# Three edits to a two-layer decoder trunk: gating products on GpSimd, v's first loads issued later, two sets of PSUM banks at the end

## The chip, the cores and the metric

The kernel runs on one core of a Trainium2 chip. The metric is the device time of one execution in microseconds (us), lower is better. A profiled execution gives a trace: what each engine did and when, counted from the start of its span. The engines are PE (TensorE, the matrix multiplier; its weight loads are listed as PEld), DVE (VectorE), ACT (ScalarE), POOL (GpSimd) and SP (SyncE, which here only issues DMAs). Each engine takes its own instructions strictly in the order in which the program was built.

## The reference

Two layers over a residual stream `x` of 1024 positions by 2048 channels, all in float32. Cut to what is computed:

```python
for layer in range(2):
    mod = silu(c) @ w_mod[layer] + b_mod[layer]            # 2048 x 6144, a matrix-vector product
    shift, scale, gate = split(mod, 3)
    h = rms_norm(x, ln_pre_g[layer]) * (1 + scale) + shift
    y = ab_mixer(h) if layer == 0 else ssm_mixer(h)
    x = x + gate * rms_norm(y, ln_post_g[layer])

def ab_mixer(h):                                           # layer 0
    a_u, a_v, a_z, q, k, v, b_z = split(h @ w_in, 7)       # 2048 x 7168
    # 8 gating heads: chunks of 128 positions mixed by a masked 128 x 128 matrix
    vh = rms_norm(gelu(a_v) per head);  s = tril(w_s) @ vh + b_s
    out_a = gelu(a_u) * s * silu(a_z)
    # 8 stick-breaking attention heads, strictly causal
    z = q k^T / sqrt(128);  later = reversed cumulative sum of log_sigmoid(-z)
    out_b = (exp(log_sigmoid(z) + later) masked) @ v * silu(b_z)
    return concat(out_a, out_b) @ w_out                    # 2048 x 2048

def ssm_mixer(h):                                          # layer 1
    u, z = split(h @ w_in, 2)                              # 2048 x 2048
    y = S5 state space of u (64 groups of 16 channels, 64 complex states) + d * u
    g = gelu(y);  y = g * sigmoid(g @ w_glu + b_glu)       # 1024 x 1024
    return (y * silu(z)) @ w_out                           # 1024 x 2048
```

## The kernel before, in words

Every large product is done with three matmuls (`mm3`, L209 to L212): each float32 operand is split into a high part (ACT copies it to fp32r, `whi`) and a remainder (DVE subtracts, `wlo`), by `split` (L186, L187). `gemm` (from L214) walks over the contraction: `load_w` takes a raw weight tile `wraw` from a ring of four, splits it, and four PSUM banks accumulate. In the last step the banks are finished one after the other, and `evac` empties each. The banks come from `mm_tile`, a set of four, unless the caller hands in `tiles`.

The order of the work. A scheduler builds the instruction order of each engine from the program text, from priorities (`hi_prio`) and from its own timeline; `tc.issue_after(x)` keeps instructions behind `x` in that order, and `tc.manual_schedule` keeps the written order on the engines it names. The stages are:

1. Modulation of layer 0 and the first projections (up to about 146 us). SP loads four x tiles `xa` of 1 MB, then `w_mod` in pieces of 1 MB (`ring` and `raw`, L371; two pieces make up what one round of `sums`, L380, needs) and the first weights `fraw`. PE forms the modulation row from these, ACT and DVE turn it into the normalised, transposed `hTh` and `hTl` (high and low), and PE runs the first three projections (`first`).
2. Eight heads (to about 1600 us). Each head `h` has projections (`v`, `qk`, `uz`, `bz`), the stick-breaking attention, and a gating head. `proj_v(0, 0)` (L466) is the first of the projections of v. `gate_a(h)` runs the silu and gelu functions on ACT and then calls `sgu_out(h)` (L545): the product `sg` times `u` (L547), then that times `zg` into `u` in another order of its elements (L548), then a store to `cat_d` (L550). In heads 0 to 2 the rest of the modulation (`mod_chunk`) is done beside it on DVE, in heads 3 to 7 the preparation of the S5 matrices (`s5_prep`), whose products are on POOL (L1159, L1162), its transposes and small matmuls on PE (`wb_ps` L1285, `k_ps` L1298).
3. Output projection of layer 0 (`o0e`, `o1e`), projections of layer 1, S5 blocks.
4. The two last stages: the GLU product (`glue`, four column groups, each with eight split weights), and the output projection of layer 1 (`out0e` with four column groups of 512, `out1e` with three, and `outr`, the fourth for the last four row blocks, kept apart so that each row block ends with its own normalisation `post` and store). `outr` takes its weights from `wres`, split once.

In the last stage `evac` (L963) empties a bank twice: DVE multiplies it by the gains into `y` (L965), ACT squares it for the norm (`jk`, L967).

Of the kernel before, what the change touches and what calls it, by code (L numbers as in the profile page):

```python
# [63 lines left out]
def hybrid_trunk(ctx: ExitStack, tc: tile.TileContext, x, c, ln_pre_g, ln_post_g, w_mod, b_mod,  # L64
# [10 lines left out]
    def pool(name, bufs=1, **kw):  # L75
        return tc.tile_pool(name=name, bufs=bufs, reuse_waits="tile", **kw)
# [10 lines left out]
    def big_tile(i, shape, dt, name):  # L87
        return big[i].tile(shape, dt, tag="big", name=name)
# [183 lines left out]
    def perm(t):  # L272
        return t.rearrange("p (j n) -> p n j", j=8)
# [40 lines left out]
    with pool("p0") as p0:  # L314
# [148 lines left out]
        hTh[1] = big_tile(1, [128, KT, 512], F32R, "hTh1")  # L463
        hTl[1] = big_tile(1, [128, KT, 512], F32R, "hTl1")
        new_v()
        proj_v(0, 0)  # L466
        xbank = [ps_z.tile([128, 512], F32, tag="z", name="xT") for _ in range(2)]
        with hi_prio():
            for k in range(KT):
# [6 lines left out]
    with pool("pa") as pa, pool("pst") as pst, pool("pat", 2) as pat, ExitStack() as pm_stack:  # L476
# [67 lines left out]

        def sgu_out(h):  # L545
            u, z, s = st["u"], st["z"], st["s"]
            V.tensor_tensor(out=s, in0=s, in1=u, op=ALU.mult)  # L547
            V.tensor_tensor(out=perm(u), in0=s.rearrange("p (n j) -> p n j", j=8),  # L548
                            in1=z.rearrange("p (n j) -> p n j", j=8), op=ALU.mult)
            dma(out=cat_d[h], in_=u)  # L550

# [152 lines left out]
    def proj_z(cg, halves, pre=None):  # L704
# [12 lines left out]
        o = 1024 + cg * 256  # L717
        gemm(KT, 256, lambda k0, k1: [(0, 0, wi[:, k0:k1, o:o + 256])], banks, evac, f"sz{cg}e", pre)

    with pool("pb") as pb:  # L720
        gg = pb.tile([128, D], F32, name="gg0")
        dma(out=gg, in_=gg_d[0].partition_broadcast(128))
# [6 lines left out]
        def load_cat(hf, k):  # L729
            with hi_prio():  # L730
                raw = load_raw(kord(catv, k, slice(hf * 512, (hf + 1) * 512)), 512)
                split(catH[hf][:, KORD[k], :], catL[hf][:, KORD[k], :], raw)

        def other_banks(name):

            return [p_.tile([128, 512], F32, tag=tag, name=name)
                    for p_, tag in ((ps_z, "z"), (ps_z, "z"), (ps_t, "t"), (ps_o, "o"))]

        def h1_turn(hf, ys, ks):

# [172 lines left out]
    with pool("pe") as pe:  # L913
        wg = w_glu[0].rearrange("(k p) n -> p k n", p=128)
        zs = []
        tab.begin("sigm")
        for k in range(8):
            zt = pe.tile([128, L], F32, tag="zt", name="zt", bufs=8)
            dma(out=zt, in_=z_d[k])
            gt = pe.tile([128, L], F32, tag="gt", name="gt", bufs=2)  # L920
            dma(out=gt, in_=g_d[k])
            G.tensor_tensor(out=gt, in0=gt, in1=zt, op=ALU.mult)  # L922
            tab.act(zt, zt, AF.Sigmoid)
            V.tensor_tensor(out=zt, in0=zt, in1=gt, op=ALU.mult)
            zs.append(zt)
        for cg in range(4):
            def evac(b, ps, cg=cg):
                cb, hf = divmod(b, 2)
                k = cg * 2 + cb
                s = slice(hf * 512, (hf + 1) * 512)  # L930
                sg = pe.tile([128, 512], F32, tag="sgm", name="sgm", bufs=3)
                tab.act(sg, ps, AF.Sigmoid, bias=BGLU[:, k:k + 1])
                V.tensor_tensor(out=sg, in0=sg, in1=zs[k][:, s], op=ALU.mult)
                split(yTh[:, k, s], yTl[:, k, s], sg)

            banks = []
            for cb in range(2):
                for hf in range(2):
                    def f(k, wh, wl, cb=cb, hf=hf):
                        s = slice(cb * 128, (cb + 1) * 128)  # L940
                        t = slice(hf * 512, (hf + 1) * 512)
                        return wh[:, s], wl[:, s], gT[0][:, k, t], gT[1][:, k, t]
                    banks.append((512, f))
            gemm(8, 256, lambda k0, k1, cg=cg: [(0, 0, wg[:, k0:k1, cg * 256:(cg + 1) * 256])], banks, evac, "glue")
        tab.begin("explog")


    with pool("pd") as pd:
        gg = pd.tile([128, D], F32, name="gg1")
        dma(out=gg, in_=gg_d[1].partition_broadcast(128))  # L950
        wo2 = w_out_ssm[0].rearrange("(k p) n -> p k n", p=128)
        outv = out[0].rearrange("(n j) d -> j n d", j=8)

        def op_out(k, wh, wl, j):
            s = slice(j * 128, (j + 1) * 128)
            return yTh[:, k, s], yTl[:, k, s], wh, wl

        for hf in range(2):
            js = range(hf * 4, hf * 4 + 4)
            ys = [pd.tile([128, D], F32, tag="y", name="y1", bufs=4) for _ in js]  # L960
            ssq = pd.tile([128, 4, 4], F32, tag="ssq", name="ssq1", bufs=2)

            def evac(b, ps, ng, ys=ys, ssq=ssq):  # L963
                n0 = ng * 512
                V.tensor_tensor(out=ys[b][:, n0:n0 + 512], in0=ps, in1=gg[:, n0:n0 + 512], op=ALU.mult)  # L965
                jk = pd.tile([128, 512], BF16, tag="jk", name="jk1")
                S.activation(jk, ps, AF.Square, accum_out=ssq[:, b, ng:ng + 1])  # L967

            def post(b, n, ys=ys, ssq=ssq, js=js, hf=hf):
                tot = pd.tile([128, 1], F32, tag="tot", name="tot1", bufs=2)  # L970
                V.tensor_reduce(out=tot, in_=ssq[:, b, :], axis=mybir.AxisListType.X, op=ALU.add)
                r = rstd_from(tot, 1, D, pd, "ry")
                for q in range(D // n):
                    qs = slice(q * n, (q + 1) * n)
                    xr = pd.tile([128, 1024], F32, tag="xr", name="xr1", bufs=4)[:, 0:n]
                    dma(out=xr, in_=x1_d[js[b]][:, qs])
                    o = ys[b][:, qs] if hf else xr
                    V.scalar_tensor_tensor(out=o, in0=ys[b][:, qs], scalar=r, in1=xr, op0=ALU.mult, op1=ALU.add)
                    (G.dma_start if n > 512 else dma)(out=outv[js[b]][:, qs], in_=o)

            for ng in range(4 if hf == 0 else 3):
                banks = [(512, lambda k, wh, wl, j=j: op_out(k, wh, wl, j)) for j in js]
                gemm(8, 512, lambda k0, k1, ng=ng: [(0, 0, wo2[:, k0:k1, ng * 512:(ng + 1) * 512])], banks,
                     lambda b, ps, ng=ng, evac=evac: evac(b, ps, ng), f"out{hf}e")
            if hf == 0:
                for b in range(4):
                    post(b, 1024)
            else:
                wres = big_tile(0, [128, 2, 8, 512], F32R, "wres")
                for k in range(8):  # L990
                    with hi_prio():
                        raw = load_raw([(0, 0, wo2[:, k:k + 1, 1536:2048])], 512)
                        split(wres[:, 0, k, :], wres[:, 1, k, :], raw)
                for b, j in enumerate(js):
                    ps = mm_tile("outr")
                    for k in range(8):
                        mm3(ps, *op_out(k, wres[:, 0, k, :], wres[:, 1, k, :], j), k == 0, k == 7)
                    evac(b, ps, 3)
                    post(b, 1024 if b < 3 else 512)
# [344 lines left out]
```

## Time and profile before

| | |
|---|---|
| median of 3 runs | 2652.79 us (2651.98 to 2653.84) |
| the profiled execution | 2647.22 us |
| its span | 2645.5 us |
| PE busy | 2581.9 us, 98% of the span |
| DVE busy | 1556.2 us, 59% |
| ACT busy | 1017.9 us, 38% |
| POOL busy | 373.2 us, 14% |
| mean granted TensorE clock | 0.997 of full |

The profiled execution is one of its own, 5.6 us under the median of the others, and 1.7 us of it lie outside the span. A busy PE need not be a fast one, since matmuls overlap, but where PE is listed idle nothing of the kernel's main work goes on. So the idle time of PE and what released it is what to read. Idle time of the other engines costs nothing by itself.

### The profile page before, as it was taken

Reading aid. Unit: us, or ns where it says so; the run is one execution under the profiler, and the core shown is the slowest. Engines: PE = TensorE matmul, PEld = TensorE weight load, DVE = VectorE, ACT = ScalarE, POOL = GpSimd, SP = SyncE. Lnnn points to the kernel's source line nnn. Section 1 sums busy time; section 2 is a strip of 40 time slices with the busy share of each in tenths; the row PEclk is TensorE's granted clock in tenths of the full one; section 3 lists DMA queues with packets and bytes.
Section 4 is the critical chain, followed back from the end, with each engine's and each line's share of the span. In section 5 each row is a group of like instructions: output and inputs, shape, how many; then the busy total and the mean of one; then the engine's idle time right before and its main releaser. Section 6 shows DMA issues by size and latency. Waiting matters only on the chain.

```text
span 2645.5 us, 40197 instructions
## 1 busy us (share of the span) xinstructions
PE 2581.9 (98%) x14107; PEld 2171.6 (82%) x14107; DVE 1556.2 (59%) x3613; ACT 1017.9 (38%) x2021; POOL 373.2 (14%) x692
## 2 busy tenths in 40 slices
PE   5999999999999999999999999999999999999998
PEld 3788988988989878778889777887888888887886
DVE  1244676676756766855847664455264676646354
ACT  3384524235315315234334353444253322134333
POOL 0000101000000260631713400013013000002000
PEclk9999999999999999999999999999999999999999
DMA  9935283772752241422413435453364675463354
GB/s 348 382 92 173 65 262 107 235 251 61 250 182 73 64 117 52 129 70 76 127 50 113 108 96 187 160 201 102 96 218 148 207 229 182 139 213 137 132 204 169
DMA packets 373050, 410.75 MB, mean 155 GB/s; under 512 B 30032, under 2 KB 269424, under 8 KB 371568
## 3 DMA queue, kind: packets, MB, share of 16 engines
q1 hardware_dynamic: 364480, 390.28, 46.5%
q0 software_dynamic: 8160, 17.84, 2.0%
q8 instruction: 111, 1.82, 0.3%
q14 instruction: 91, 0.75, 0.1%
q10 hardware_dynamic: 208, 0.07, 0.0%
HBM read 348.28 MB, written 59.79 MB: 154 GB/s over the span
## 4 chain that ended last, share of the span: by engine, by line
PE 73%; issue 9%; DVE 7%; DMA 6%; ACT 3%; SPq 1%; POOL 1%; DVEq 0%; ACTq 0%; POOLq 0%
PE z L564 2%; PE oT L592 2%; PE o1e L210 2%; PE o1e L211 2%; PE o1e L212 2%; DVE wlo L187 1%; PE out0e L212 1%; PE out0e L210 1%; PE out0e L211 1%; PE su1e L210 1%; PE su1e L212 1%; PE su1e L211 1%; PE mrow L380 1%; PE su0e L210 1%; PE su0e L212 1%
## 5 line engine op out<-in xcount | busy, mean ns | idle before, releaser
L186 ACT ACTIVATE whi<-wraw 128x512 fp32r<-128x512 f32 x608 | 381.2, 630 | 928.3 <-PE o1e L212 87.3
L187 DVE TENSOR_TENSOR wlo<-wraw,whi 128x512 fp32r<-128x512 f32 x608 | 429.4, 709 | 480.2 <-ACT whi L186 469.1
L180 DVE SCALAR_TENSOR_TENSOR macc<-mraw,cond,macc 128x512 f32<-128x512 f32 x240 | 180.1, 751 | 77.4 <-DMA mraw<-in_w_mod_dram 73.1
L56 ACT ACTIVATE sp<-sp 128x128 f32<-128x128 f32 (+3 forms) x192 | 99.5, 520 | 3.6
L210 PE MATMUL o1e<-whi,catH 128*128 128x512 f32 x256 | 99.2, 391 | 1.4 <-ACT jk L765 1.4
L210 PE MATMUL o0e<-whi,catH 128*128 128x512 f32 x256 | 100.1, 391 | 0.0
L211 PE MATMUL o0e<-wlo,catH 128*128 128x512 f32 x256 | 100.0, 391 | 0.0
L212 PE MATMUL o1e<-whi,catL 128*128 128x512 f32 x256 | 99.8, 390 | 0.0
L211 PE MATMUL o1e<-wlo,catH 128*128 128x512 f32 x256 | 99.8, 390 | 0.0
L212 PE MATMUL o0e<-whi,catL 128*128 128x512 f32 x256 | 99.7, 390 | 0.0
L56 ACT ACTIVATE sp<-z 128x128 f32<-128x128 f32 (+3 forms) x96 | 46.8, 488 | 118.5 <-PE z L564 118.3
L526 POOL DMA_DIRECT2D sw<-in_sgu_w_dram x8 | 4.7, 586 | 575.9 <-PE sgw L530 380.5
L592 PE MATMUL oT<-wT,v 128*128 128x128 f32 x576 | 80.4, 275 | 5.6 <-DVE wT L590 5.6
L592 PEld LDWEIGHTS oT<-wT,v 128*128 128x128 f32 x576 | 75.1, 191 | 9.8 <-DVE wT L590 6.9
L564 PE MATMUL z<-k,q 128*128 128x128 f32 (+3 forms) x192 | 77.4, 486 | 0.0
L569 DVE SCALAR_TENSOR_TENSOR sp<-z,sp 128x128 f32<-128x128 f32 (+3 forms) x96 | 52.9, 551 | 40.9 <-ACT sp L56 40.9
L922 POOL TENSOR_TENSOR gt<-gt,zt 128x1024 f32<-128x1024 f32 x8 | 20.5, 2571 | 385.1 <-DMA gt<-g_d 379.0
L56 ACT ACTIVATE wt<-wt 128x128 f32<-128x128 f32 (+3 forms) x96 | 50.2, 522 | 58.0 <-DVE wt L581 54.8
L590 DVE COPY wT<-wT_ps 128x128 f32<-128x128 f32 (+3 forms) x96 | 53.1, 553 | 26.8 <-PE wT_ps L588 26.2
L802 POOL DMA_DIRECT2D x_d<-y x32 | 17.6, 550 | 345.9 <-DVE y L799 331.5
L1288 ACT ACTIVATE s5wb<-wb_ps 128x128 f32<-128x128 f32 x64 | 17.7, 276 | 126.3 <-DVE s5wb L1287 96.6
L571 POOL TENSOR_SCALAR_AFFINE_SELECT sp<-sp 128x128 f32<-128x128 f32 x64 | 22.8, 356 | 259.5 <-DVE sp L569 242.6
(627 smaller groups left out, 7924.6 us busy)
## 6 DMA issues: line engine op xcount, KB each, us to landing
wraw<-in_w_in_ab_dram SPq DMA_DIRECT2D x528, 128.0 KB, 2.5
mraw<-in_w_mod_dram SPq DMA_DIRECT2D x256, 256.0 KB, 3.8
wraw<-in_w_out_ab_dram SPq DMA_DIRECT2D x128, 256.0 KB, 3.1
wraw<-in_w_in_ssm_dram SPq DMA_DIRECT2D x112, 256.0 KB, 3.4
ring<-in_w_mod_dram SPq DMA_DIRECT2D x16, 1024.0 KB, 10.9
raw<-in_w_mod_dram SPq DMA_DIRECT2D x16, 1024.0 KB, 9.7
wraw<-in_w_out_ssm_dram SPq DMA_DIRECT2D x64, 256.0 KB, 3.3
wraw<-in_w_in_ab_dram SPq DMA_DIRECT2D x32, 256.0 KB, 2.8
```

The costliest lines, as they stand in the source:

```text
L56: r = self.nc.scalar.activation(out, in_, func, **kw)
L180: V.scalar_tensor_tensor(out=acc, in0=m, scalar=cond[:, k:k + 1], in1=acc, op0=ALU.mult, op1=ALU.add)
L186: S.activation(h, r, AF.Copy)
L187: eng.tensor_tensor(out=lo, in0=r, in1=h, op=ALU.subtract)
L210: T.matmul(ps, sh, mh, start=first, stop=False)
L211: T.matmul(ps, sh, ml, start=False, stop=False)
L212: T.matmul(ps, sl, mh, start=False, stop=last)
L380: T.matmul(prow[32 * j:32 * j + 32], condb[:, kk, :], m[:, k + j % 2, :], start=kk < 2, stop=kk >= KT - 2)
L564: T.matmul(z[:, :w], q[:, i * 128:(i + 1) * 128], kT[:, k0:k1], start=True, stop=True)
L569: V.scalar_tensor_tensor(out=a[:, :w], in0=z[:, :w], scalar=0.0, in1=a[:, :w], op0=ALU.max, op1=ALU.add)
L590: V.tensor_copy(wT[:, :w], pt[:, :w])
L592: T.matmul(oT, v[:, k0 // 128 + j, :], wT[:, j * 128:(j + 1) * 128], start=nb_done == 0, stop=nb_done == i)
```

## The change

It has three parts. First, `proj_v(0, 0)` is put behind the last load of `w_mod` of the modulation stage. Second, the two products of `sgu_out` are issued on POOL instead of DVE (`G` instead of `V`). Third, in the two last stages every other column group takes its banks from the pools `ps_z`, `ps_t` and `ps_o` (`other_banks`, which moves to an outer place); `wres` is loaded and split during the second column group of `out1e` instead of behind the third; `outr` uses the other banks; and in `evac` ACT's square is issued ahead of DVE's product.

```diff
         new_v()
-        proj_v(0, 0)
+        with tc.issue_after(st["last"].ins):
+            proj_v(0, 0)
...
         def sgu_out(h):
             u, z, s = st["u"], st["z"], st["s"]
-            V.tensor_tensor(out=s, in0=s, in1=u, op=ALU.mult)
-            V.tensor_tensor(out=perm(u), in0=s.rearrange("p (n j) -> p n j", j=8),
+            G.tensor_tensor(out=s, in0=s, in1=u, op=ALU.mult)
+            G.tensor_tensor(out=perm(u), in0=s.rearrange("p (n j) -> p n j", j=8),
                             in1=z.rearrange("p (n j) -> p n j", j=8), op=ALU.mult)
             dma(out=cat_d[h], in_=u)
...
+    def other_banks(name):
+
+        return [p_.tile([128, 512], F32, tag=tag, name=name)
+                for p_, tag in ((ps_z, "z"), (ps_z, "z"), (ps_t, "t"), (ps_o, "o"))]
...
-            gemm(8, 256, lambda k0, k1, cg=cg: [(0, 0, wg[:, k0:k1, cg * 256:(cg + 1) * 256])], banks, evac, "glue")
+            gemm(8, 256, lambda k0, k1, cg=cg: [(0, 0, wg[:, k0:k1, cg * 256:(cg + 1) * 256])], banks, evac, "glue",
+                 tiles=other_banks("glue") if cg % 2 else None)
...
                 n0 = ng * 512
-                V.tensor_tensor(out=ys[b][:, n0:n0 + 512], in0=ps, in1=gg[:, n0:n0 + 512], op=ALU.mult)
                 jk = pd.tile([128, 512], BF16, tag="jk", name="jk1")
                 S.activation(jk, ps, AF.Square, accum_out=ssq[:, b, ng:ng + 1])
+                V.tensor_tensor(out=ys[b][:, n0:n0 + 512], in0=ps, in1=gg[:, n0:n0 + 512], op=ALU.mult)
...
+            if hf:
+                wres = big_tile(0, [128, 2, 8, 512], F32R, "wres")
+
+            def load_res(k):
+
+                with hi_prio():
+                    raw = load_raw([(0, 0, wo2[:, k:k + 1, 1536:2048])], 512)
+                    split(wres[:, 0, k, :], wres[:, 1, k, :], raw)
+
             for ng in range(4 if hf == 0 else 3):
...
-                     lambda b, ps, ng=ng, evac=evac: evac(b, ps, ng), f"out{hf}e")
+                     lambda b, ps, ng=ng, evac=evac: evac(b, ps, ng), f"out{hf}e",
+                     load_res if hf and ng == 1 else None, tiles=other_banks(f"out{hf}e") if ng % 2 else None)
...
-                wres = big_tile(0, [128, 2, 8, 512], F32R, "wres")
-                for k in range(8):
-                    with hi_prio():
-                        raw = load_raw([(0, 0, wo2[:, k:k + 1, 1536:2048])], 512)
-                        split(wres[:, 0, k, :], wres[:, 1, k, :], raw)
+                spare = other_banks("outr")
                 for b, j in enumerate(js):
-                    ps = mm_tile("outr")
+                    ps = spare[b]
```

Since a scheduler sets the order, the change moves more than its lines. SP's queue at the start of the program, and (below the line of dots) where the modulation's loads end; `wraw` are v's weights, `xb` the second half of x:

```order
-L136 DMA xa<-in_x_dram 128x2048
-L195 DMA wraw<-in_w_in_ab_dram 128x2x128 x5
-L136 DMA xa<-in_x_dram 128x2048
-L195 DMA wraw<-in_w_in_ab_dram 128x2x128 x3
-L136 DMA xa<-in_x_dram 128x2048 x2
+L1348 UNCONDITIONAL_BRANCH
+L136 DMA xa<-in_x_dram 128x2048 x4
 L371 DMA ring_144<-in_w_mod_dram 128x8x256 x4
...
 L371 DMA raw_143<-in_w_mod_dram 128x8x256 x4
+L195 DMA wraw<-in_w_in_ab_dram 128x2x128 x8
 L460 DMA xb<-in_x_dram 128x2048 x4
```

The eight loads of v leave the place between the x tiles and stand behind the last `w_mod` load, ahead of `xb`.

POOL's queue in the fourth head, before, where the S5 preparation has begun (`s5Tr`, `s5Ti`, `s5cAr` and `s5cAi` are what PE transposes or multiplies, `s5cl` a load for the next groups):

```order
L1162 TENSOR_TENSOR s5Tr_7884<-s5Tr_7884,s5tb_7886 128x128
L1159 TENSOR_TENSOR s5tb_7886<-s5pw_7580,s5bbr_7871 128x128
L1162 TENSOR_TENSOR s5Ti_7885<-s5Ti_7885,s5tb_7886 128x128
L1232 DMA s5cl_8151<-in_c_re_dram 16x2x64 x4
L1232 DMA s5cl_8151<-in_c_im_dram 16x2x64 x2
L1159 TENSOR_TENSOR s5cAr_7887<-s5pw_7580,s5cT_7865 128x144
```

and the same place after the change (numbers of lines are 8 higher there):

```order
L1167 TENSOR_TENSOR s5tb_7886<-s5pw_7580,s5bbr_7871 128x128
L1170 TENSOR_TENSOR s5Ti_7885<-s5Ti_7885,s5tb_7886 128x128
L548 TENSOR_TENSOR sg<-sg,u 128x1024
L1240 DMA s5cl_8151<-in_c_re_dram 16x2x64 x4
L1240 DMA s5cl_8151<-in_c_im_dram 16x2x64 x2
L1167 TENSOR_TENSOR s5cAr_7887<-s5pw_7580,s5cT_7865 128x144
L1167 TENSOR_TENSOR s5tb_7886<-s5pw_7580,s5cT_7865 128x144
L1167 TENSOR_TENSOR s5cAi_7888<-s5pw_7580,s5cT_7865 128x144
...
L1240 DMA s5cl_8151<-in_c_im_dram 16x2x64 x2
L549 TENSOR_TENSOR u<-sg,zg 128x128x8
```

The two products of the gating head now stand within the chain of the S5 preparation, the first ahead of the loads `s5cl`, the second behind them. The sixth head has them in such a place too; in the other heads they stand between the masks of the attention or at the edge of the S5 work.

ACT's queue before, where `out1e` goes over into `outr`:

```order
L186 ACTIVATE whi<-wraw 128x512
L967 ACTIVATE jk_24975,ssq_24668<-out1e 128x512
L967 ACTIVATE jk_24981,ssq_24668<-out1e 128x512
L967 ACTIVATE jk_24987,ssq_24668<-out1e 128x512
L186 ACTIVATE whi<-wraw 128x512 x4
L186 ACTIVATE wres<-wraw 128x512 x8
L967 ACTIVATE jk_25129,ssq_24668<-out1e 128x512
```

After the change nothing of `wres` is left there; its eight copies stand in the second column group, in turn with those of `whi`.

## Rows read from the trace of the kernel before

**Rows 1.** The page's busy time of the engines: busy us (share) and instructions.
```profile
PE 2581.9 (98%) x14107; PEld 2171.6 (82%) x14107; DVE 1556.2 (59%) x3613; ACT 1017.9 (38%) x2021; POOL 373.2 (14%) x692
```

**Rows 2.** Waits of PE: line, released by, us in total, times, longest.
```profile
PE mrow L380 <- DMA ring<-in_w_mod_dram: 17.4, 2, 15.7
PE glue L210 <- ACT sgm L56: 1.8, 2, 1.5
```

**Rows 3.** Timeline of PE, first 48 us: start, us, instruction [idle before, released by].
```profile
24.47 3.64 PE L380 MATMUL mrow<-ring,condb 128*32 128x256 f32 x32 [15.67 <-DMA ring<-in_w_mod_dram]
...
39.72 3.64 PE L380 MATMUL mrow<-raw,condb 128*32 128x256 f32 x32 [2.02 <-DMA raw<-in_w_mod_dram]
...
47.59 1.93 PE L380 MATMUL mrow<-raw,condb 128*32 128x256 f32 x32
```

**Rows 4.** Timeline of PE behind those products: two of five such gaps.
```profile
667.84 1.05 PE L164 MATMUL cs<-ones,macc 128*128 128x1 f32 x8 [1.10 <-DVE wT L590]
...
1586.78 1.16 PE L592 MATMUL oT<-wT,v 128*128 128x128 f32 x8 [2.25 <-DVE wT L590]
```

**Rows 5.** Timeline of PE in the last stage, its two gaps.
```profile
2567.52 0.50 PE L210 MATMUL out1e<-whi,yTh 128*128 128x512 f32 x1 [1.13 <-ACT jk L967]
...
2612.71 0.50 PE L210 MATMUL outr<-wres,yTh 128*128 128x512 f32 x1 [1.37 <-ACT jk L967]
```

**Rows 6.** DMA issues of the first 12 us: queue, count, KB each, us to landing.
```profile
wraw<-in_w_in_ab_dram SPq DMA_DIRECT2D x8, 128.0 KB, 5.1
```

**Rows 7.** Timeline of SP's DMA issues, first 22 us.
```profile
1.26 5.37 SPq L195 DMA_DIRECT2D wraw<-in_w_in_ab_dram  x5
6.91 0.34 SPq L136 DMA_DIRECT2D xa<-in_x_dram  x1
7.30 1.63 SPq L195 DMA_DIRECT2D wraw<-in_w_in_ab_dram  x3
...
9.96 11.67 SPq L371 DMA_DIRECT2D ring<-in_w_mod_dram  x4
```

**Rows 8.** Stretches of the start; the last three columns: clock, DMA share, GB/s.
```profile
4.00:8.00 4.00, 0.00 (x0) 0.00 (x0) 0.00 (x0) 2.00 (x2) 0.00 (x0) 1.00 0.92 280
8.00:12.00 4.00, 0.45 (x1) 0.18 (x1) 0.29 (x1) 0.00 (x0) 0.00 (x0) 1.00 0.92 307
...
20.00:24.47 4.47, 0.00 (x0) 0.03 (x1) 2.82 (x7) 3.37 (x6) 0.00 (x0) 1.00 1.09 386
...
29.79:39.72 9.93, 5.76 (x45) 2.99 (x45) 3.39 (x8) 4.83 (x8) 0.00 (x0) 0.84 1.11 373
```

**Rows 9.** The two products: ns min/median/max, and what DVE waited for (us, times).
```profile
L547 DVE TENSOR_TENSOR sg<-sg,u x8: 1224/1226/1226, 326.4 to 1584.6; 128x1024 f32<-128x1024 f32 x8
...
  ACT u L56: 26.7, 8
```

**Rows 10.** The same of the second product.
```profile
L548 DVE TENSOR_TENSOR u<-sg,zg x8: 1955/2021/2046, 328.1 to 1586.6; 128x1024 f32<-128x1024 f32 x8
```

**Rows 11.** Timeline of DVE around the last head's products.
```profile
1584.62 1.23 DVE L547 TENSOR_TENSOR sg<-sg,u 128x1024 f32<-128x1024 f32 x1 [4.84 <-ACT u L56]
1585.76 0.37 DVE L596 TENSOR_TENSOR bz<-oT,bz 128x128 f32<-128x128 f32 x1
1586.04 0.68 DVE L590 COPY wT<-wT_ps 128x512 f32<-128x512 f32 x1
```

**Rows 12.** The only products of this size on POOL, in the GLU stage.
```profile
L922 POOL TENSOR_TENSOR gt<-gt,zt x8: 2368/2400/3346, 2377.4 to 2414.5; 128x1024 f32<-128x1024 f32 x8
```

**Rows 13.** Timeline there, of DVE and of POOL.
```profile
2389.91 0.69 DVE L187 TENSOR_TENSOR yTl<-sgm,yTh 128x512 fp32r<-128x512 f32 x1
2390.51 2.89 DVE L187 TENSOR_TENSOR wlo<-wraw,whi 128x512 fp32r<-128x512 f32 x1
...
2390.43 5.23 POOL L922 TENSOR_TENSOR gt<-gt,zt 128x1024 f32<-128x1024 f32 x2 [6.08 <-DMA wraw<-in_w_glu_dram]
```

**Rows 14.** Timeline of the fourth head: POOL's S5 chain, then PE's use of it.
```profile
913.74 2.17 POOL L1232 DMA_DIRECT2D s5cl<-in_c_re_dram  x4 [7.48 <-PE c_ps L1235]
...
927.21 0.42 POOL L1159 TENSOR_TENSOR s5tb<-s5pw,s5bi 128x128 f32<-128x128 f32 x1 [4.55 <-DVE s5cAi L1280]
...
928.98 0.41 PE L1298 MATMUL k_ps<-s5cAr,s5bd 128*32 128x128 f32 x2
```

**Rows 15.** The chain that ended last, its end: start, us, what.
```profile
2618.22 0.24 PE outr L212
...
2635.05 5.47 DMA xr<-x_d
2640.55 0.75 DVE y L978
```

More of the change, by code (lines that the diff above doesn't have):

```diff
@@ L732, in load_cat @@
                 split(catH[hf][:, KORD[k], :], catL[hf][:, KORD[k], :], raw)
-        def other_banks(name):
-            return [p_.tile([128, 512], F32, tag=tag, name=name)
-                    for p_, tag in ((ps_z, "z"), (ps_z, "z"), (ps_t, "t"), (ps_o, "o"))]
         def h1_turn(hf, ys, ks):
```

## The prediction

> **What bounds the kernel now.** I read the page's busy times first: PE is busy for 2581.9 of 2645.5 us, POOL for 373.2 [rows 1]. So a change can win only where PE is idle, some 64 us in all, or lose by making it idle. The waits of PE say for whom: most is the start, where the modulation's first matmul waits 15.67 us for `w_mod` [rows 2, 3]. Then I looked for the gaps that the three parts of the change touch: five in the heads behind the gating products [rows 4], two in `glue` of 1.8 us together [rows 2], and two in the last stage [rows 5]. The reader is to see that all of them are small beside the start, where DMA is what ends last.
>
> **Part 1, v's first loads.** Eight DMAs of 128 KB, 1.05 MB in all [rows 6], leave the place between the x tiles, and SP issues `w_mod` from 9.96 us on only because 5.37 + 1.63 us before that go to them [rows 7]. The first sums then start at 24.47 us, when their data land [rows 3]. Later the queue moves 386 GB/s [rows 8], so the bytes alone are worth 1.05 MB / 386 GB/s = 2.7 us: the lower end. The upper end is the 7.0 us of issuing. In between: from 4 to 12 us the queue moved 280 and 307 GB/s, while v's loads were in it [rows 8], some 92 GB/s x 8 us = 0.74 MB below its later rate, another 1.9 us. That makes 4.6 us, and I take 4.5.
>
> Does it last? The sums of the second round, at 39.72 us, wait for DMA as well [rows 3], with the queue at 373 GB/s in between [rows 8] and the same loads in it; so they move by the same amount. From then on the page shows PE without a wait for DMA, and everything moves with it. The normalisation of x keeps up, since its own loads come earlier too. v's loads now stand ahead of `xb`, but there they have the time of the last rounds, when both are long under way before PE is done with `first`; I cost that at nothing, and it would cost 2.7 us if `xb` were what PE waits for. One thing stays open: the rounds at 24.47 and 39.72 us take 3.64 us, the one at 47.59 us 1.93 us [rows 3], TensorE being at its lower clock level (mean granted 0.84 between 29.79 and 39.72 us [rows 8]) behind its idle time. If the earlier data move that stretch, 1.7 us come or go with it.
>
> **Part 2, the products on POOL.** Each head takes 1.23 and 2.02 us from DVE [rows 9, 10], and before them DVE stands still until the gelu of `u` is done, 26.7 us over eight [rows 9]: 52.7 us, or 6.6 us a head, in which nothing else on DVE's queue goes on. Five gaps of PE follow such a block, of 0.70 to 2.25 us and 6.2 us together, of which two are shown [rows 4]. In the last head one sees how: DVE waits 4.84 us, does one product, and only then copies the `wT` that PE needs [rows 11]. If all five go, 6.2 us are won.
>
> What comes instead? On POOL a product of this size takes 2.40 us [rows 12]. The second one writes a strided output, which on DVE makes 2.02 out of 1.23 us; on POOL the trace shows no such operation, so between 2.40 and 2.40 x 2.02 / 1.23 = 3.9 us. I take 2.40, the nearest row. Off the path that costs nothing: `s` and `u` are written again only after the next projections, and what stands behind the products on POOL's queue, the load `sw` and the masks of the next attention, is wanted after those as well; SP's store to `cat_d` moves with them. But DVE isn't freed for good: a `wlo` that ran beside such a POOL product took 2.89 us instead of 0.69 [rows 13]. So each of the 16 products may hold one DVE instruction for up to 2.2 us, 4.4 us a head in place of 6.6 us. If the gaps shrink in that ratio, 6.2 x (1 - 4.4/6.6) = 2.1 us are won, and I take that.
>
> The Trainium skill speaks against this part: GPSIMD Engine Reference, section "Performance versus the Vector engine", gives 1.96 times DVE's time for such a product, and section "Specifications" says that the SBUF interfaces are shared with VectorE where it reads two SBUF inputs. The trace agrees with both: 2.40 against 1.23 us, and the 2.89 us. By that rule alone DVE would lose what it wins, and part 2 would be worth nothing; that is the first rival below.
>
> The lower end of part 2 is a loss. In the fourth and sixth head the products stand within the S5 preparation on POOL. There POOL had 4.55 us of slack once, behind `s5cAi` [rows 14], but PE's `k_ps` follows only 1.8 us behind the end of that wait [rows 14], so a later POOL soon makes PE wait. Two products of 2.40 to 3.9 us in the way are up to 6.4 us a head, 12.8 us in both; against the 6.2 us won, that is 6.6 us lost at worst.
>
> **Part 3, the last stages.** The gaps before `glue`, 1.8 us [rows 2], and before `out1e` and `outr`, 1.13 and 1.37 us [rows 5], each wait for ACT to empty the first bank of the set that the next group reuses. With another set they need not wait: 4.3 us at most, and I take 4.0, for the rest that a new order leaves. `wres` costs the same eight copies and remainders, moved into a group in which ACT and DVE then do two of each for every step of the contraction. A step there is twelve matmuls of 0.24 us [rows 15], 2.9 us, and two loads of 128 x 512 float32, 0.52 MB in that time, are 181 GB/s, under half of the 386 that the queue moves at the start [rows 8]. If the four raw tiles run short there, PE waits again, and part 3 is worth nothing: its other end is 0. Issuing ACT's square ahead of DVE's product changes only who reads the bank first: nothing. The end, from `outr` over the last load of `xr`, 5.47 us, to the last product of DVE [rows 15], hangs on PE's row blocks and moves with them.
>
> **The sum.** 4.5 + 2.1 + 4.0 = 10.6 us. The profiled execution has 2647.22 us and would have 2636.6; the median of the runs stands 5.6 us above it, at 2652.79, and goes to 2642.2 us.
>
> **The rivals.**
> 1. *The shared port eats part 2.* DVE waits for POOL as long as it worked before, the five gaps stay. For it speaks the 2.89 us [rows 13]; against it that the copy `wT<-wT_ps` before PE's gap [rows 11] reads PSUM and a stretched instruction of that kind isn't in the trace. 4.5 + 4.0 = 8.5 us: 2644.3 us.
> 2. *The new order costs half of it back.* Every head from the third on is scheduled anew, so gaps can open anywhere, and each product that a gap of today hangs on gets new neighbours. Five new gaps like today's five, 6.2 us, leave 10.6 - 6.2 = 4.4 us: 2648.4 us, which is no change. For it speaks that PE waits for so many different releasers in the heads, `cs` and `oT` [rows 4] among them; against it that the scheduler's order of today leaves such small ones.
> 3. *Slower: the S5 preparation is held up.* POOL's products wait for gelu, 26.7 / 8 = 3.3 us each head, and take 4.8 to 6.3 us; in the four heads with S5 work behind them that is 4 x 8.1 to 4 x 9.6, 32 to 38 us, by which the transposes and small matmuls on PE's queue could come late, and PE is in order. It decides from the point at which more than 8.5 + 5.3 = 13.8 us of it reach PE, 3.5 us a head. With half, 17.5 us: 2652.8 - 8.5 + 17.5 = 2661.8 us. Against it: in two of the four the new order has the products at the edge of the S5 work, not in it.
> 4. *The change doesn't do what it says*: v's loads could still be issued early. The order shows them behind, so I give it nothing.
>
> **How the numbers follow.** What this kernel's measurement can tell from no change is about 0.2%, 5.3 us: faster is below 2647.5, slower above 2658.1. The forecast has 0.45, and the first rival 0.25; both are faster. The second has 0.20, of which I count 0.17 as no change and 0.03 as faster; the third 0.10, of which 0.08 is slower and 0.02 no change. So faster 0.73, same 0.19, slower 0.08. The likeliest one's own range: part 1 from 2.7 to 7.0, part 2 from -1 to 6.2, part 3 from 2 to 4.3, hence 2652.8 - 17.5 to 2652.8 - 3.7, 2635.3 to 2649.1 us. Toward the low end all three parts would have to be at their best, so I leave it at 2635; upward the range goes to 2654, which leaves the third rival out and a little below.
>
> **What would show it.** Right: the first `mrow` sums start near 20 us instead of 24.47; the gaps of PE before `glue`, `out1e` and `outr` are gone; the two products stand on POOL at 2.4 us, and gaps behind `wT` are fewer; POOL's busy time is 38 to 50 us up. Wrong: sums at 22 us or later (part 1 too large); `wlo` or `macc` of up to 2.9 us beside the products, with a PE gap behind (rival 1); `wb_ps` or `k_ps` waiting for POOL by several us in the fourth to seventh head (rival 3); PE waiting for `whi` or `wlo` in the second group of `out1e`.

## The result and the profile after

The changed kernel is slower: 2666.97 us median (2662.82 to 2669.43) against 2653.32 us of the kernel before measured beside it (four runs each), ratio 1.0051 with a 95% interval of 1.0036 to 1.0066. The forecast was 2642.2 us, so it has the wrong sign. The profiled execution took 2669.32 us, span 2667.5, which is 22.0 us of span above the one of before; it lies at the upper end of its runs and the one of before below all of its own, so its sums overstate the loss of the medians, 13.6 us.

The page's busy times of the kernel after, which answer to [rows 1]:

```profile
PE 2593.6 (97%) x14107; PEld 2179.5 (82%) x14107; DVE 1563.2 (59%) x3597; ACT 1015.7 (38%) x2021; POOL 411.6 (15%) x708
```

PE is busy for 11.7 us more with the same 14107 matmuls, and the rest of the 22 us, some 10 us, is idle time. POOL took on 38.4 us, the low end of the forecast. DVE lost two products a head, 26 us, and is still 7.0 us *busier* than before. Its other instructions have been stretched by 33 us in sum if those 26 us are taken off, and by 25 us against run 10 below, which leaves both products out (DVE busy 1538.1 us).

PE's waits by what released them (us in total, times, longest), after:

```profile
PE cols_ps L138 <- DMA rows<-in_b_glu_dram: 11.8, 1, 11.8
PE mrow L380 <- DMA ring<-in_w_mod_dram: 9.4, 2, 7.2
PE cs L164 <- DVE macc L180: 7.2, 4, 2.5
PE oT L593 <- DVE wT L591: 5.2, 2, 4.0
PE wb_ps L1293 <- DVE s5tp L1025: 3.0, 4, 0.9
PE k_ps L1308 <- DVE s5cAi L1288: 2.7, 2, 2.1
PE gate_ps L164 <- DVE macc L180: 1.9, 3, 0.7
...
PE out1e L210 <- ACT whi L186: 1.2, 3, 0.9
```

and before, rows not shown so far:

```profile
PE cols_ps L138 <- DMA rows<-in_b_glu_dram: 8.4, 1, 8.4
...
PE oT L592 <- DVE wT L590: 5.6, 4, 2.2
...
PE cs L164 <- DVE wT L590: 1.1, 1, 1.1
PE wb_ps L1285 <- DVE s5fin L1020: 1.0, 1, 1.0
PE k_ps L1298 <- DVE bz L596: 0.9, 1, 0.9
...
PE cs L164 <- DVE macc L180: 0.4, 1, 0.4
```

The waits at `glue`, `out1e <- jk` and `outr` [rows 2, 5] are gone, and so are 8.0 us of the 17.4 for `w_mod`, of which `cols_ps` at the very start takes back 3.4. But `oT`, which the products' move was to help, has lost hardly anything in sum, and `cs`, `gate_ps`, `wb_ps` and `k_ps` have grown by 10.4 us (5.1 before, 15.5 after, over all their releasers). These are the column sums of the modulation in heads 0 to 2, and the S5 preparation. PE's timeline after, at the places of [rows 3, 4] and at the new gaps:

```profile
19.52 3.23 PE L380 MATMUL mrow<-ring,condb 128*32 128x256 f32 x32 [7.25 <-DMA ring<-in_w_mod_dram]
...
34.78 3.64 PE L380 MATMUL mrow<-raw,condb 128*32 128x256 f32 x32 [1.84 <-DMA raw<-in_w_mod_dram]
...
555.89 1.05 PE L164 MATMUL cs<-ones,macc 128*128 128x1 f32 x8 [2.13 <-DVE macc L180]
...
693.90 1.21 PE L164 MATMUL cs<-ones,macc 128*128 128x1 f32 x8 [2.46 <-DVE macc L180]
...
1277.51 0.41 PE L1308 MATMUL k_ps<-s5cAi,s5bd 128*32 128x128 f32 x2 [2.14 <-DVE s5cAi L1288]
```

Both rounds of sums start 4.9 us earlier (24.47 and 39.72 us before). How far PE is ahead of or behind before at fixed points of the program tells where the time went: 4.24 us ahead at the first `v1e` (269.39 us before), 8.66 behind at the first `bz4e` (861.35), 21.65 behind at the first `o1e` (1751.22), and 22.12 at the end of `outr`. So heads 0 to 2 lose 12.9 us and heads 3 to 7 (with `o0e`, which ends there) another 13.0, and the stages behind change little in sum.

What DVE does before such gaps, in its timeline after:

```profile
542.07 2.33 DVE L180 SCALAR_TENSOR_TENSOR macc<-mraw,cond,macc 128x512 f32<-128x512 f32 x3 [0.96 <-DMA mraw<-in_w_mod_dram]
...
550.68 5.15 DVE L180 SCALAR_TENSOR_TENSOR macc<-mraw,cond,macc 128x512 f32<-128x512 f32 x4 [2.42 <-DMA mraw<-in_w_mod_dram]
...
667.67 2.48 DVE L187 TENSOR_TENSOR wlo<-wraw,whi 128x512 fp32r<-128x512 f32 x1 [3.93 <-ACT whi L186]
670.07 0.68 DVE L591 COPY wT<-wT_ps 128x512 f32<-128x512 f32 x1
670.67 2.26 DVE L187 TENSOR_TENSOR wlo<-wraw,whi 128x512 fp32r<-128x512 f32 x1
```

and POOL's:

```profile
667.20 2.40 POOL L548 TENSOR_TENSOR sg<-sg,u 128x1024 f32<-128x1024 f32 x1 [9.14 <-ACT u L56]
669.68 2.71 POOL L549 TENSOR_TENSOR u<-sg,zg 128x1024 f32<-128x1024 f32 x1
...
1252.94 0.46 POOL L1170 TENSOR_TENSOR s5Tr<-s5Tr,s5tb 128x128 f32<-128x128 f32 x1
1255.00 2.41 POOL L548 TENSOR_TENSOR sg<-sg,u 128x1024 f32<-128x1024 f32 x1 [1.60 <-ACT u L56]
1257.36 0.43 POOL L1167 TENSOR_TENSOR s5tb<-s5pw,s5bbr 128x128 f32<-128x128 f32 x1
```

The two `wlo` beside the products take 2.48 and 2.26 us, not 0.69, while the copy of `wT` out of PSUM between them keeps its 0.68. Four `macc` take 5.15 us beside the second head's products, where three take 2.33 without. The Trainium skill (SBUF — State Buffer, section "Who interferes with whom") says that a DVE instruction with two SBUF inputs contends with a GpSimd instruction that reads SBUF. The trace agrees, with these numbers. In the sixth head POOL waits 1.60 us for gelu and then does 2.41 us of product, while S5's next product stands behind; the step from `s5Tr` to `s5tb` was 0.08 us before:

```profile
1241.48 0.46 POOL L1162 TENSOR_TENSOR s5Tr<-s5Tr,s5tb 128x128 f32<-128x128 f32 x1
1242.02 0.42 POOL L1159 TENSOR_TENSOR s5tb<-s5pw,s5bbr 128x128 f32<-128x128 f32 x1
```

PE's longer busy time goes with its clock. Stretches of the kernel after, three of them, and one of run 9 below; the column behind the busy times is the granted clock:

```profile
558.11:561.52 3.41, 3.41 (x10) 2.67 (x9) 3.38 (x7) 0.00 (x0) 0.00 (x0) 0.50 0.80 246
1616.24:1619.65 3.41, 3.35 (x13) 3.16 (x14) 1.90 (x4) 1.67 (x3) 0.00 (x0) 0.50 0.28 95
1827.87:1834.70 6.83, 5.26 (x15) 3.88 (x16) 5.57 (x8) 3.75 (x9) 6.83 (x7) 0.50 0.00 0
...
1806.83:1813.66 6.83, 5.38 (x14) 4.04 (x15) 4.76 (x7) 2.88 (x8) 6.83 (x7) 0.50 0.00 0
```

Each of the three new gaps above is followed by 3.41 us at 0.50, which is 1.2 GHz (from 558.11, 694.64 and 1278.32 us); a fourth such stretch begins at the end of a gap of 3.96 us at 1616.30, and one of 6.83 us lies at the gaps of `h1T`. Together 20.5 us at half speed, up to 10.2 us of work. The kernel before has no such stretch between its start and its end in the profile shown. But that profile is the odd one: run 1 has 3.4 us of them there, run 4 6.8, run 3 10.2, run 10 13.7 and run 9, the fastest, 17.1 us, all without a product moved to POOL, and their PE is busy for 2.3 to 5.4 us more than before. So what the clock adds to the loss is less than these two profiles say.

### The profile page after: what moved, and what is told of

It reads as the page before. It is cut to its first block, busy times and chain, and to the rows that moved or that the text cites. A ratio compares the mean times of both kernels' runs of the same rounds, so it can differ in the third digit from the quotient of the medians.

```text
span 2667.5 us, 40202 instructions
## 1 busy us (share of the span) xinstructions
PE 2593.6 (97%) x14107; PEld 2179.5 (82%) x14107; DVE 1563.2 (59%) x3597; ACT 1015.7 (38%) x2021; POOL 411.6 (15%) x708
## 5 line engine op out<-in xcount | busy, mean ns | idle before, releaser
L187 DVE TENSOR_TENSOR wlo<-wraw,whi 128x512 fp32r<-128x512 f32 x608 | 445.0, 734 | 484.6 <-ACT whi L186 476.7
L572 POOL TENSOR_SCALAR_AFFINE_SELECT sp<-sp 128x128 f32<-128x128 f32 x64 | 23.8, 371 | 259.0 <-DVE sp L570 256.7
```

Source lines behind the costliest of these rows:

```text
L187: eng.tensor_tensor(out=lo, in0=r, in1=h, op=ALU.subtract)
L572: G.affine_select(out=a[:, w - 128:w], in_=a[:, w - 128:w], pattern=[[-1, 128]], base=0, channel_multiplier=1, compare_op=ALU.is_gt, fill=0.0)
```

## The experiments

Two theories stood at the start. A: the products on POOL cost the time, and parts 1 and 3 gain. B: part 1's early start is given back in the heads. Later the cost of part 2 was divided between O, the order made anew (with the products gone from DVE the scheduler puts PE's `cs` earlier), and C, POOL working beside DVE.

"Lost" is how far PE falls back against before between the first `v1e` and the first `bz4e` (heads 0 to 2), and from there to the first `o1e` (heads 3 to 7), one profile each; `o0e` is counted with heads 3 to 7. Six profiles whose order in heads 0 to 2 is that of before lost 0.0 to 3.6 us there (1, 3, 4, 6, 9 and 12), so less than that says nothing. Three with the products on POOL there in one and the same order lost 10.5 to 13.9 (2, 5 and after).

| run | products on POOL | median us, before beside it | ratio, 95% | lost, heads 0-2 | lost, heads 3-7 |
|---|---|---|---|---|---|
| after | all | 2666.97, 2653.32 | 1.0051 (1.0036-1.0066) | 12.9 | 13.0 |
| 1 part 1 | none | 2646.67, 2652.75 | 0.9975 (0.9964-0.9986) | 0.2 | 1.7 |
| 2 part 2 | all | 2674.47, 2652.75 | 1.0077 (1.0056-1.0099) | 13.9 | 12.0 |
| 3 part 3 | none | 2651.50, 2652.75 | 0.9994 (0.9983-1.0004) | 3.6 | 1.0 |
| 4 parts 1, 3 | none | 2645.10, 2652.75 | 0.9965 (0.9954-0.9975) | 2.2 | 2.1 |
| 5 heads 0-2 | 3 heads | 2661.42, 2652.03 | 1.0037 (1.0024-1.0050) | 10.5 | 3.2 |
| 6 heads 3-7 | 5 heads | 2664.15, 2652.03 | 1.0043 (1.0027-1.0059) | 2.9 | 14.7 |
| 7 added | added | 2667.55, 2652.03 | 1.0058 (1.0042-1.0073) | 9.8 | 6.6 |
| 8 in pieces | all, in pieces | 2676.86, 2652.03 | 1.0090 (1.0075-1.0106) | 14.4 | 13.4 |
| 9 late column | none | 2640.43, 2652.97 | 0.9955 (0.9942-0.9967) | 0.0 | 1.7 |
| 10 left out | none at all | 2651.21, 2652.97 | 0.9991 (0.9981-1.0001) | 4.4 | -2.9 |
| 11 one of two | half | 2663.34, 2652.97 | 1.0041 (1.0028-1.0055) | 6.7 | 9.5 |
| 12 behind S5 | 5 heads | 2661.19, 2651.91 | 1.0035 (1.0021-1.0049) | 0.1 | 12.0 |

**1 to 4: each part by itself.** All on the kernel before; 1 is the first hunk of the diff, 2 the second, 3 the others, 4 is 1 and 3:

```
1: +with tc.issue_after(st["last"].ins):
       proj_v(0, 0)
2: -V.tensor_tensor(out=s, ...)        +G.tensor_tensor(out=s, ...)
   -V.tensor_tensor(out=perm(u), ...)  +G.tensor_tensor(out=perm(u), ...)
3: +tiles=other_banks("glue") if cg % 2 else None      (also out0e, out1e, outr)
   +load_res if hf and ng == 1 else None
   ...
```

> Only part 1: v's first loads behind the modulation, everything else as before. Theory A (the products on POOL alone cost the time): the first sums start near 19.5 us, the 4.2 us that are left of it at 269 us stay to the end, 2653.3 - 4.2 = 2649 us. Rival B (the early start is given back in the heads): in the changed kernel PE waited for macc before gate_ps and cs with an order that was still that of before, 3.8 us between 331 and 541 us; if the modulation's later loads set that pace, the same waits are here, and the time is 2652 to 2653 us.

> Only part 2: the two products of each head on POOL. Theory A: the changed kernel lost 26 us between 265 and 1773 us, all of it by the products: 2653.3 + 26 = 2679 us, with gaps of PE at k_ps, wb_ps, cs and oT and several stretches of 3.41 us at the lower clock. Rival B: 3.8 us of it belong to part 1's early start, so 2653.3 + 22 = 2675 us, with no waits at gate_ps. Rival C (the three parts hurt together only, by a new order): 2651 to 2656 us.

> Only part 3: two sets of PSUM banks in the last two stages, the early last column of W, and ACT's square ahead of DVE's product. By the changed kernel's rows PE gains 2.4 us at glue, loses 1.1 in out1e and gains 1.7 at outr: 2653.3 - 3.0 = 2650.3 us (theory A). Rival: the last loads of the residual set the end anyway, and the gain is under 1 us: 2652.5 us or more.

> Parts 1 and 3 together, the products on DVE. Theory A: 2653.3 - 4.2 - 3.0 = 2646 us, and the half-clock stretches in the heads are gone. Rival B (part 1 given back in the heads): 2650 us.

Part 1 gains 6.1 us by the medians, part 2 loses 21.7, part 3 gains 1.3, which its interval doesn't tell from nothing. The sum, 14.3 us slower, is what was measured for all three, 13.6. Part 1 and part 3 together gain 7.7. Theory A holds. B falls: in run 1 PE loses 0.2 us in heads 0 to 2, and run 2, though its 2674.5 us is B's number rather than A's, still waits 1.5 us at `gate_ps`. One sign of A failed: run 4, with no product on POOL, has two stretches at 0.50 in the heads all the same (663.98 and 1585.57 us). Part 3 is short of its 3.0 us, and PE's waits in run 3 show where; below them one of the four, with the copy on ACT that ends it:

```profile
PE out1e L210 <- ACT whi L186: 4.3, 4, 1.7
...
2579.20 0.63 ACT L186 ACTIVATE whi<-wraw 128x512 fp32r<-128x512 f32 x1 [1.49 <-DMA wraw<-in_w_out_ssm_dram]
...
2579.89 1.19 PE L210 MATMUL out1e<-whi,yTh 128*128 128x512 f32 x4 [1.70 <-ACT whi L186]
```

ACT is idle there and waits for the raw tile's load, as it does before three of the four `whi` (1.49, 2.00 and 2.75 us); SP in turn holds loads until DVE's `wlo` gives a raw tile back (21.8 us between 2540 and 2625 us).

**5 and 6: which heads.**

```
+E = G if h < 3 else V      (run 6: h > 2)
+E.tensor_tensor(out=s, ...); E.tensor_tensor(out=perm(u), ...)
```

> Part 2 alone, but with the products on POOL in heads 0 to 2 only, those that also compute the modulation. In the run of part 2 alone PE was 13.9 us behind at the end of v4e (861 us) and another 12 us behind at o0e. If the two stretches have causes of their own, this one costs the first alone: 2653 + 14 = 2667 us. Rival: the first stretch only moves later work into a bad place, and without products in heads 3 to 7 some is caught up: 2660 us or less.

> Part 2 alone, with the products on POOL in heads 3 to 7 only, those with the S5 preparation. Theory (POOL's queue and the order of the S5 work): 2653 + 12 = 2665 us, with the waits at k_ps, wb_ps, c_ps and oT as in part 2 alone, and no wait at cs above those of before. Rival (the loss hangs on the modulation heads): under 2 us, 2655 us or less.

9.4 and 12.1 us by the medians, together 21.5 against part 2's 21.7. So there are two losses that add up, one beside the modulation and one beside the S5 preparation. Run 6 came out as expected, but for `cs`, which waits 1.8 us for `macc` against 0.4 before. Run 5 is nearer to its rival's 2660 us than to 2667, but its profile shows nothing caught up later: it has lost 10.5 us in heads 0 to 2 instead of 13.9, a difference that equal orders show as well.

**7: POOL beside DVE, with the order of before.**

```
 V.tensor_tensor(out=perm(u), ...)
+G.tensor_tensor(out=z, in0=s, in1=z, op=ALU.mult)
+G.tensor_tensor(out=perm(z), in0=s, in1=s, op=ALU.mult)     (both in the strided views)
```

> The kernel before, products on DVE, with two products of the same size and form added on POOL behind them in each head, which write z when nothing reads it any more. The order of PE and DVE is that of before up to the qk projection of head 4, so in heads 0 to 2 only the shared access and POOL's queue are tested. Theory O (the new order costs it: PE's cs stands 12 to 21 matmuls earlier than macc can be done): PE is within 1.5 us of before at the end of v4e. Theory C (the shared port: each POOL product holds one DVE instruction for some 2 us): PE is 10 us or more late there, as with part 2. For the end of the run: O 2653 to 2658 us, C 2670 us.

PE lost 9.8 us in heads 0 to 2, far above theory O's 1.5 and near C's 10, with the order of PE and DVE unchanged up to the qk projection of head 4. The time is up by 15.5 us. DVE's and PE's timelines of this run, in the second head:

```profile
553.85 2.71 DVE L187 TENSOR_TENSOR wlo<-wraw,whi 128x512 fp32r<-128x512 f32 x1
556.48 2.38 DVE L180 SCALAR_TENSOR_TENSOR macc<-mraw,cond,macc 128x512 f32<-128x512 f32 x1
```

```profile
560.49 1.05 PE L164 MATMUL cs<-ones,macc 128*128 128x1 f32 x8 [2.91 <-DVE macc L180]
```

Two instructions are held, 2.0 us by the first and 1.6 by the second, and PE stands 2.91 us at the column sums of the same chunk. In the profile of before there is little slack at this place, 0.35 us from the end of the last `macc` to `cs`:

```profile
556.14 0.75 DVE L180 SCALAR_TENSOR_TENSOR macc<-mraw,cond,macc 128x512 f32<-128x512 f32 x1
...
557.24 0.95 PE L164 MATMUL cs<-ones,macc 128*128 128x1 f32 x8
```

At the other column sums right behind a `macc` it is 0.1 to 1.5 us, and 3.05 once, so most of what holds `macc` reaches PE. Summed over heads 0 to 2, DVE's instructions took 9.9 us more in this run than the medians of the same forms before, about what PE lost; 8.6 in run 2, 3.6 in run 11, and nothing in the runs without POOL's products there.

**8: the products in pieces.**

```
+for p in range(4):  c = slice(p * 256, (p + 1) * 256)
+    G.tensor_tensor(out=s[:, c], in0=s[:, c], in1=u[:, c], op=ALU.mult)
+for p in range(4):  (the strided product likewise, 32 columns of n each)
```

> Part 2 alone, with each product on POOL cut into four of 256 columns, so that none can hold a DVE instruction for longer than some 0.7 us; PE's cs stands as early as with part 2 in the first chunks. Theory O (order): the loss up to the end of v4e stays, 10 us or more, and the time is near 2670 us. Theory C (port): the held instructions go, most of the loss with them: 2660 us or less.

By the medians it loses 24.8 us against part 2's 21.7, with intervals that overlap, so the pieces are no better. The expectation of C fails, but its premise failed too: the holding was halved and not gone (4.6 us in heads 0 to 2 by the same sum), and SP waits longer. SP's timeline of this run in the first head:

```profile
334.08 0.34 SPq L554 DMA_DIRECT2D cat_d<-u  x1
334.51 1.20 SPq L195 DMA_DIRECT2D wraw<-in_w_in_ab_dram  x2
335.80 0.99 SPq L497 DMA_DIRECT2D mraw<-in_w_mod_dram  x2
```

A piece takes 0.74 us at the median and the eight of this head 6.7, so `u` is done later, and SP, which is in order, holds the loads of `wraw` and `mraw` behind the store of `u`. The store stood at 330.19 us before and at 332.91 in run 2. DVE's `wlo` beside these pieces took 0.81 us, a `macc` 1.31. That half the holding cost as much, 14.4 us in heads 0 to 2, speaks for a second cause there, the order or the later loads; this run leaves open which.

**10 and 11: relief without POOL, and half the products.** Run 10 leaves both products out on every engine, so its output lacks the gating; run 11 moves the first alone.

```
10: -V.tensor_tensor(out=s, ...)   -V.tensor_tensor(out=perm(u), ...)
11: -V.tensor_tensor(out=s, ...)   +G.tensor_tensor(out=s, ...)
```

> The kernel before without the two products of each head, on any engine (the gated output is left out: u goes to cat_d as gelu leaves it). It shows what DVE's relief is worth with nothing on POOL in return, the upper end of part 2. Theory P (the prediction's): the five gaps go, 6.2 us, 2646 us. Theory O (the order made anew costs by itself, whatever POOL does): 2656 us or more, with PE waiting at cs, which stands 2 to 6 matmuls earlier in three chunks. Theory R (most of the loss is POOL beside DVE): between 2645 and 2653 us.

> Only the first of the two products of a head (s times u, contiguous, 2.4 us) on POOL, the second stays on DVE behind it. If the loss goes with the time that POOL works beside DVE, 2.4 of 5.1 us a head, it is half of part 2's 22 us: 2663 us. If it comes from the order made anew, it is about the whole: 2670 us or more. DVE waits for POOL here, so up to 2.4 us a head may come on top of the half, where nothing else on DVE's queue covers it.

Without any product the kernel gains 1.8 us, within its uncertainty, not 6.2; that is in theory R's range. The five gaps of the prediction are gone, in this run all of them, but others opened. PE's waits of run 10:

```profile
PE cs L164 <- DVE macc L180: 3.5, 5, 1.1
PE oT L589 <- DVE wT L587: 2.7, 1, 2.7
```

The wait at `oT` is not the one of 2.25 us [rows 4] but the next in the same head, 1.52 us before. DVE's timeline in run 10 shows what is late now:

```profile
1595.15 0.69 DVE L187 TENSOR_TENSOR catL<-wraw,catH 128x512 fp32r<-128x512 f32 x1 [1.52 <-ACT catH L186]
1595.76 0.68 DVE L587 COPY wT<-wT_ps 128x512 f32<-128x512 f32 x1
```

The copy of `wT` stands behind a remainder that waits for ACT: DVE is in order, and the free time was given to work of the next stage (three such remainders between the two copies of `wT`, two before). In heads 0 to 2 the free time went into waiting for loads. What DVE waits for ahead of `macc` (us, times, longest), before, in run 10 and after:

```profile
DVE macc L180 <- DMA mraw<-in_w_mod_dram: 73.1, 77, 2.3
DVE macc L180 <- DMA mraw<-in_w_mod_dram: 84.8, 79, 3.1
DVE macc L180 <- DMA mraw<-in_w_mod_dram: 92.0, 80, 3.3
```

The two products of three heads are 9.7 us of DVE; the wait grew by 11.7 without them. It grew by 18.9 in the changed kernel; how much of that is freed time and how much loads that come late isn't separated. `cs` stands 2 to 6 matmuls earlier in three chunks and waits 3.5 us for `macc` instead of 0.4 (with part 2, 12 to 21 matmuls earlier): part of theory O is real. In heads 0 to 2 run 10 (its order alone) lost 4.4 us and run 7 (POOL alone) 9.8, together 14.2; part 2 lost 13.9. That sum proves little: the 4.4 are just outside what equal orders lost, 3.6 at most, and no run has part 2's own order without POOL, so O's share in part 2 isn't known. Run 11 lost 10.4 us by the medians with 2.4 us of POOL a head, part 2 21.7 with 5.1: that is the half of its first expectation, the loss going with the time that POOL works, and not the 2670 us of an order made anew.

**12: products out of gelu's way.** In heads 3 to 7 the products wait in POOL's queue until the S5 work of the head is issued.

```
+tab.pool = G.tensor_tensor(...)                  (S5's own products and sums)
+with tc.issue_after(tab.pool.ins) if h > 2 else nullcontext():
+    E.tensor_tensor(out=s, ...); E.tensor_tensor(out=perm(u), ...)
```

> Products on POOL in heads 3 to 7 only, but in POOL's queue behind the S5 work of the head's pieces, so that they come long after gelu and POOL never stands waiting for it with S5 work behind. In the run with these heads PE lost 14.7 us between the ends of v4e and o0e; products beside an order that doesn't wait for gelu lost 6.6 us there. Theory Q (POOL waiting for gelu holds up the S5 work): 6 to 7 us are left, 2657 us. Rival R (any 5 us of POOL's time in the S5 chain costs as much, wherever it stands): 2664 us as before.

12.0 us are lost instead of 14.7, and the time is 9.3 us above before instead of 12.1, with intervals that overlap. POOL's own wait for gelu ahead of the products fell from 39.4 to 10.2 us, all of it in the last head, so that hold is gone, but PE's waits of this run have new names:

```profile
PE sgw L530 <- ACT s5wb L1290: 3.5, 2, 2.3
PE oT L594 <- DVE wT L592: 3.4, 1, 3.4
```

2661.19 us (2657.5 to 2664.9 by the interval) lies between Q's 2657 and R's 2664, nearer to R: most of the loss doesn't hang on POOL's wait for gelu. Whether there the held DVE or POOL's own queue weighs more stays open, since the S5 preparation uses both. In these heads the runs don't add up either: run 10 (-2.9) and run 7 (6.6) make 3.7, part 2 lost 12.0.

**9: the version that beats both.** Parts 1 and 3, products on DVE, and the last column of W loaded behind the third group, as before:

```
-load_res if hf and ng == 1 else None
+for k in range(8):  raw = load_raw(... 1536:2048 ...); split(wres[:, 0, k, :], wres[:, 1, k, :], raw)
 spare = other_banks("outr")
```

> Parts 1 and 3 with the products on DVE, but the last column of W is loaded and split where it was before, behind the third group of out1e, instead of inside the second. In the runs of part 3 PE waited for whi inside out1e, 4.3 and 3.4 us. Theory (two raw tiles a step are too many there): these waits go, glue keeps its 2.4 us and outr its 1.2 to 1.5, so with part 1's 6 us the time is 2652.5 - 6 - 3.5 = 2643 us. Rival (the sets of banks bring nothing once the column is late, since ACT empties the banks as late): 2646 us, as part 1 alone.

2640.43 us, ratio 0.9955 with 0.9942 to 0.9967: 12.5 us faster than before (8.8 to 15.4 by the interval, which holds the theory's 2643 us and not the rival's 2646). In its profile PE has no wait left in `glue`, `out1e` and `outr`, and from the first `glue` to the end of `outr` it takes 5.5 us less than before. With part 1's 6.1 us that is 11.6 of the 12.5.

Against run 4, 4.7 us by the medians for the column alone; the intervals overlap, so what is shown is that the waits for `whi` went.

## Why the prediction was wrong

**Part 1, right and a little small.** Forecast 4.5, measured 4.9 us at both rounds, and 6.1 by the medians of run 1. The clock is listed at 0.50 between 25.63 and 39.28 us, before between 36.52 and 43.35; the second round takes 3.64 us in both, so nothing came or went by it there. For the round at 24.47 us, which the prediction put at the lower level too, the profile lists 1.00, so that its 3.64 us are the clock's isn't shown.

**Part 2, wrong, and nearly the whole error lies here: -2.1 us forecast, +21.7 measured, 23.8 of the 24.8 us by which the median missed.** The failed step is "If the gaps shrink in that ratio, 6.2 x (1 - 4.4/6.6) = 2.1 us". Both sides of it fail.
- *The gain.* That the five gaps hang on DVE's products is right: in run 10 all five are gone. That they would be won is wrong, since the order is made anew with it and other instructions come late, `cs`, `c_ps` and the next `oT`, and since in heads 0 to 2 DVE then waits for `mraw` instead; run 10 gains 1.8 us, with nothing on POOL. In the changed kernel `oT`'s waits are 5.2 us in place of 5.6.
- *The cost.* The 4.4 us a head of held DVE instructions was right as a bound: the 25 to 33 us of stretching are 3 to 4 us a head, the two `wlo` of the third head lose 3.4 us, the `macc` of the second some 2. But it was weighed only against DVE's freed time, as if both lay off the path. DVE's `macc` is what PE's column sums wait for, with little to spare: in run 7, with an unchanged order, 3.6 us of held DVE became a wait of 2.91 us, and three heads lost 9.8 us. What held instructions cost in heads 3 to 7 no run separates from POOL's queue and the order. The lower end of part 2, 6.6 us lost, counted only the S5 work of two heads and nothing in the modulation heads; the range then took -1 us for it, and with the -6.6 it would have ended near 2654.7.
- *What was priced at nothing.* The clock in the heads: stretches at 0.50 stand behind the new gaps, worth up to 10.2 us in the profiled execution. Since runs without POOL's products have up to 17.1 us of such stretches, worth up to 8.5, how much of the 21.7 us they make isn't shown.

The rule of the Trainium skill that the prediction weighed (GPSIMD Engine Reference, section "Specifications") holds in this trace, with the 2.48 and 2.26 us. The step from the stretched instructions to "worth nothing" was the prediction's own, and left out who waits for the held engine.

**Rival 3 was the nearest, with a chance of 0.10.** Its mechanism, S5 work behind POOL's products, is in the trace (1255.00 us), and heads 3 to 7 lost 13.0 us; its price of 17.5 us was not far off for them. But that is in part luck: run 12 takes most of POOL's wait for gelu away and still loses 12.0 us there, so which part of the mechanism costs stays open, and it left out heads 0 to 2. Rival 2 (a new order opens gaps like those it closes) is what run 10 shows, about 4.4 of 6.2 us. Of rival 1, the stretched instructions are right, and that they only cancel the gain is wrong.

**Part 3, right in its gaps, wrong in the column.** From stage to stage `glue` and `outr` gained 2.4 and 1.5 us, a little more than their waits of 1.8 and 1.4 us, which are gone as forecast. The forecast's other end, that the raw tiles run short and PE waits again, is what happened: 1.2 us in the changed kernel, 4.3 in run 3. 181 GB/s against 386 was the wrong test: well below the queue's rate ACT's `whi` comes late, mostly because its raw tile does, and a load waits until one of the four tiles is given back. Forecast -4.0, measured -1.3, and with the late column 5.5 us from stage to stage.

## What to carry to other kernels

A slower helper engine that shares a path with a busy one is not free because it is idle: before moving work to it, find which instructions of the busy engine will run beside it, and what the bound engine waits for in them. Test the gain first by leaving the work out altogether: here that run said 1.8 us against 6.2 us of gaps, because the freed engine was given other work in its order or waited for loads instead, and something else came late.

## What the runs showed of the hardware

- PE's clock fell to 0.50 for 3.41 us within 2.3 us behind waits of 2.13, 2.46 and 2.14 us; behind one of 2.25 us before [rows 4] the stretch from 1584.53 to 1594.00 stays at 1.00. Run 3, with the order of before in the heads, has three such stretches too (693.38, 1591.08 and 1812.95 us). So neither the wait nor the order alone decides it; it costs up to 1.7 us each time.
- A strided output costs POOL little: the second product takes 2.43 to 2.90 us, 2.72 at the median, against 2.40 of the contiguous one, where DVE needs 2.02 against 1.23 [rows 9, 10]. The prediction's 3.9 us was too high:

```profile
L549 POOL TENSOR_TENSOR u<-sg,zg x8: 2427/2715/2897, 324.7 to 1605.8; 128x1024 f32<-128x1024 f32 x8
```

- Small DVE instructions are held as well as large ones. Of three S5 products of 128x4, otherwise 0.1 us each, the first took 4.21 us beside POOL's work, after:

```profile
1262.18 4.21 DVE L1025 TENSOR_TENSOR s5tp<-s5em 128x4 f32<-128x4 f32 x1
```
